# Mixture of experts: 32 slots for the emptier experts, 96 for the two fullest, and a first bias in two single passes

## The chip, the cores and the metric

One core of one Trainium2 chip. The metric is the device time of one execution in microseconds (us), lower is better. A core has TensorE (PE, matmuls; its weight loads are listed apart as PEld), VectorE (DVE), ScalarE (ACT), GpSimd (POOL) and SyncE (SP), whose queue issues most of the DMAs.

## The reference

A network of three blocks on 256 tokens of 1024 features, float32. The change lies in the second block's mixture of experts: 32 experts, four for each token, each expert a gated product of 1024 to 2048 and a product of 1024 to 1024.

```python
logits = (xf @ w_router + b_router)
top_val, top_idx = lax.top_k(logits, TOP_K)          # 4 of 32
gates = jax.nn.softmax(top_val, axis=-1)
...
# for each expert's tokens, each with its gate:
z = x @ w_mlp1[e] + b_mlp1[e]                          # 1024 -> 2048, glu and linear interleaved
glu, lin = min(z[0::2], 7), clip(z[1::2], -7, 7)
y = (glu * sigmoid(1.702 * glu) * (lin + 1)) @ w_mlp2[e] + b_mlp2[e]
```

(The lines behind "..." are the reference's in a short form.) Evaluating the reference's router on its inputs gives the number of tokens of each expert: expert 0 has 13; the other 31 in falling order have 78, 70, 58, 55, 51, 50, 49, 45, 41, 36, 32, 32, 32, 30, 29, 28, 26, 26, 26, 25, 25, 22, 21, 20, 19, 18, 18, 16, 13, 12, 8. The place in that order, from 0 on, is the rank used below: rank 0 has 78 tokens, rank 12 has 32, rank 13 has 30.

## The kernel before

Every expert's weights are read once from HBM: 8 MB for the first product and 4 MB for the second, as twelve DMAs of 1 MB issued by SP (`load`, line 1256). They land in 14 places taken in turn: ten buffers that the whole kernel shares for raw weights (`raw`) and four of the stage's own (`wb`). A load waits in SP's queue until the products that read the place before are done. SP reads each expert's number from SBUF (line 1631) before it issues that expert's loads.

The work is static. Expert 0 comes first, as it needs no ranking, then the others in the order `order`, by ranks that the kernel works out. An expert's tokens are gathered into blocks of 64 slots; the four fullest (`FULL`) have two blocks each, one after the other against the same weights, and all the others one: 36 blocks in all. A loop of run-time length (line 1652) would take what finds no slot.

Per block: `prepare` and `dispatch` make one-hot matrices and gather the rows of four blocks at once (line 1436); `inner` adds the first bias by products of a one-hot of the expert with all the biases (line 1447, float32), then accumulates eight steps of the first product (line 1459). The 64 slots are the stationary operand, so it fills 64 columns of the array; `tile_position` puts two such halves beside each other, each with another quarter of the 2048 outputs, in two PSUM banks. Lines 1466 to 1471 apply the activation, `turned` transposes it (line 1481), `outer` does the second product, again two halves at once (line 1493), and ACT copies it to `y` (line 1496). For every two blocks `close` adds `y`, weighed by the gates, to the 1024 by 256 sums (line 1502).

A float32 product is recorded as two matmul instructions, so the first product of a block is 64 and the second 32. The compiler's scheduler orders the instructions of each engine; the PE order is fixed at build time. In between come products that belong to another stage (the memory's values, line 2449; their weights are fetched into the same places) and the second bias (line 1556). The block before the change needs `b1s`, all first biases, 256 KB, issued behind expert 0's loads (line 1295).

The layer of dense products before (`ffn`, "f11") has room for jobs that need no tokens; `router` is one of them.

Of the kernel before, what the change touches and what calls it, by code (L numbers as in the profile page):

```python
# [19 lines left out]
P = 128  # L20
T = 256
# [15 lines left out]
VALUES = 8  # the rank of the expert after which the first of the memory's values are worked out  # L37
# [4 lines left out]
class Net:  # L42
# [89 lines left out]
    # ---- tokens in, tokens out  # L132
# [51 lines left out]
    # ---- rms norm of the residual with the gain in the matmul's input and the rest left to its output  # L184
# [13 lines left out]
    def square(self, pool, p):  # L198
        """Adds the squares of two of the residual's tiles to the sums by partition."""
# [9 lines left out]
    def add_up(self, acc, tail, update, nxt, pool, fill=()):  # L209
        """The last products of the sums, two tiles of the outputs after the other, and what follows from them."""  # L210
# [12 lines left out]
    def acc_tail(self, acc, tail, p):  # L223
        """The last operand comes last: two pairs of tiles take the others first."""
# [8 lines left out]
    def first_units(self, w, tiles, n=0):  # L233
        """of the next product's first tiles, two for each chunk; the last n of them in slots of the raw weights"""
# [16 lines left out]
    def rstd_start(self):  # L251
        """of the norm that was fed, by tokens [128, 2]"""
# [39 lines left out]
    # ---- weights: raw chunks of up to 8 KB a partition, split in units of 1024 columns  # L292
# [3 lines left out]
    def raw(self, src, k, n, load=True):  # L296
        """src [k*128, n] as [128, k, n]."""
# [5 lines left out]
    def unit(self, src, slot=False):  # L303
        """src [128, a, b] in SBUF, a * b <= 1024 -> float32r parts of the same shape."""
# [12 lines left out]
    def ahead(self, makers, n):  # L317
        """Takes the makers' results in turn, each n places before it is asked for."""
# [62 lines left out]
    # ---- sum over the tiles of K as they come, all of the 1024 outputs open  # L381
# [14 lines left out]
    # ---- swiglu block: x += 0.5 * (silu(h Wg) * (h Wu)) Wo, h = rmsnorm(x)  # L396
# [104 lines left out]
    # ---- chunked spatial gating  # L501
# [89 lines left out]
    # ---- causal means over windows  # L591
    def pool_mixer(self, w_in, w_grp, scale, w_out, nxt):
        nc = self.nc
        Z = 16
        with self.tc.tile_pool(name=self.nm("pm1"), bufs=1) as p1, \
# [15 lines left out]
            # the widest windows first, as they take longest  # L611
# [33 lines left out]
            def evac(i, ps):  # L645
# [8 lines left out]
                if g:  # L654
                    # differences of the running sums
# [21 lines left out]
    # ---- conditioning: mod = silu(c) W + b, one column for each 128 features  # L677
# [43 lines left out]
    # ---- what depends on the positions alone: cos and sin of the rotations, distances of the queries' tiles to all keys  # L721
# [42 lines left out]
    def sin_reduced(self, out, x, tmp, half_out=None):  # L764
        """out = x reduced by whole turns into [-pi, pi]; |x| < 2^22."""
# [32 lines left out]
    def attn_turn(self, pool, pq, causal=True):  # L798
        """pq: probabilities of the two query tiles, [128, n] of one head, turned: keys 0 to 127 of all queries, then the others."""
# [13 lines left out]
    def attn_sum(self, pT, vv, out, causal=True):  # L813
        """out [rows, 256] = v^T p^T"""
# [4 lines left out]
    def gain(self, pool, sc, g):  # L819
        """(1 + sc) * g"""  # L820
# [4 lines left out]
    # ---- the router's matrix with the norm's gain, what the shift gives it, gain and shift by features 8 p + k  # L825
    def route_begin(self, scratch):
# [3 lines left out]
        self.turned_affine = scratch.tile([2, D], F32, name=self.nm("turned_affine"))  # L830

# [22 lines left out]
    # ---- mla and top-k sparse attention on the conditioned norm of the normed residual  # L854
    def attn2(self, V, mod, w_in, w_q_b, w_kv_b, w_o, nxt, mem):
# [6 lines left out]
        with self.tc.tile_pool(name=self.nm("at2"), bufs=2) as p2:  # L862
            # x = u * f * r1, f the first norm's gain, h = x * r2 * g * (1 + sc) + sh
# [16 lines left out]
            def wide(*runs):  # L880
                """128 columns: runs of them"""
# [14 lines left out]
            # low rank parts of the queries, keys and values, and all of the narrow ones, a step behind the input  # L896
# [35 lines left out]
            # the sparse attention's index: queries  # L932
# [16 lines left out]
            # masks: sums in the scores' own accumulation  # L949
# [60 lines left out]
            # queries: nope of two heads in a tile, rope of four  # L1010
# [36 lines left out]
            # attention of two heads at a time, its outputs in the place of the projections' input  # L1047
# [91 lines left out]
            # the last units of the first half of the ring are done with early  # L1139
# [19 lines left out]
    def post_norm(self, pool, acc, tail, g, gate=None, nxt=None, fills=((), (), ()), room=None):  # L1159
        """The last products of the sums, two tiles of the outputs after the other, and x += gate * g * rmsnorm(sums)."""  # L1160
# [76 lines left out]
    # ---- mixture of experts: 64 slots for each expert, 128 for the fullest, and a loop over blocks of 64 where they don't do  # L1237
    def moe(self, V, mod, router, w1, b1, w2, b2, nxt, ahead, mem):
        nc, tc = self.nc, self.tc
        mm = nc.tensor.matmul  # L1240
        E, S, FULL, G = 32, 64, 4, 4
# [7 lines left out]
        # all of the places for weights in turn  # L1249
# [3 lines left out]
        def load(src, n, t):  # L1253
            """one row of 2048 or two of 1024 for each partition"""
# [17 lines left out]
        with self.tc.high_priority():  # L1272
# [5 lines left out]
            iot = self.index(top, [P, S], [[1, S]], 0, 0)  # L1278
            lg = top.tile([P, 2, 40], F32, name=self.nm("lg"))
# [15 lines left out]
        nc.sync.dma_start(b1s, b1)  # L1295
        thi = self.xhi.rearrange("p j t -> p (j t)").rearrange("p (h k q) -> p h k q", h=2, k=KT)
        tlo = self.xlo.rearrange("p j t -> p (j t)").rearrange("p (h k q) -> p h k q", h=2, k=KT)
        with self.tc.high_priority():
# [6 lines left out]
            with self.behind([self.powered]):  # L1305
# [19 lines left out]
                ecol = self.index(p0, [E, 1], [[0, 1]], 0, 1)  # L1325
            for h in range(2):
                nc.vector.scalar_tensor_tensor(lg[:, h, :E], router.logits[:, h, :], r2[:, h:h + 1], self.b_route, op0=ALU.mult, op1=ALU.add)
            # the four highest, their gates, each token's place among its expert's
# [38 lines left out]
        # the last of the memory's keys in between  # L1367
# [3 lines left out]
        # experts 1 to 31 by their numbers of tokens: rank[e], perm[e, r]  # L1371
# [54 lines left out]
        with self.tc.tile_pool(name=self.nm("mo1"), bufs=1, reuse_waits="tile") as p1, \  # L1426
                self.tc.tile_pool(name=self.nm("mo2"), bufs=2, reuse_waits="tile") as p2:
            def dispatch(oh, n):
                """oh: [128, 2, n] one-hot; the chosen rows as [128, k, n]."""
# [11 lines left out]
            def inner(xe, sel, wa, hooks={}):  # L1441
                """xe(k): [128, 64]; sel: [32, 64]; the activations, two runs of 64 slots by 2 x 256."""
                chunk = lambda w, c: w.rearrange("p (q c m) -> p q c m", c=4, m=4)[:, :, c, :]
                pq = [self.bank(), self.bank()]
                for q in range(2):
                    for b in range(2):
                        mm(pq[q][64 * b:64 * b + 64, :], sel, chunk(b1s, 2 * q + b), start=True, stop=False,
                           tile_position=(0, 64 * b), skip_group_check=True)
                together = KT if callable(wa) else 4
# [1286 lines left out]
```

## Time and profile before

| | us |
|---|---|
| median of 3 runs (2836.95 to 2842.62) | 2841.77 |
| profiled execution, span from its first to its last instruction | 2844.6 |
| PE busy in it | 2720.4 (96%) |
| DVE, ACT, POOL busy | 1370.1, 927.5, 221.8 |
| stage of the experts: first load of a ranked expert issued | 1210.05 |
| its last matmul (line 1502) ends | 2317.92 |

The profiled execution has no time but its span; it lies 2.8 us (0.1%) above the median. In the rows below a group shows: line, engine, operation, output<-inputs, shapes, count, busy time in us and mean of one in ns, then idle time before it and what ended it. A busy PE isn't PE at its peak, since matmuls are pipelined and their ends modelled. In the SP rows, L1256 is the line of an expert's loads.

### The profile page before, as it was taken

Reading aid. Unit: us, or ns where it says so; the run is one execution under the profiler, and the core shown is the slowest. Engines: PE = TensorE matmul, PEld = TensorE weight load, DVE = VectorE, ACT = ScalarE, POOL = GpSimd, SP = SyncE. Lnnn points to the kernel's source line nnn. Section 1 sums busy time; section 2 is a strip of 40 time slices with the busy share of each in tenths; the row PEclk is TensorE's granted clock in tenths of the full one; section 3 lists DMA queues with packets and bytes.
Section 4 is the critical chain, followed back from the end, with each engine's and each line's share of the span. In section 5 each row is a group of like instructions: output and inputs, shape, how many; then the busy total and the mean of one; then the engine's idle time right before and its main releaser. Section 6 shows DMA issues by size and latency. Waiting matters only on the chain. (4 is left out here: it accounts for less than half of the span.)

```text
span 2844.6 us, 43953 instructions
## 1 busy us (share of the span) xinstructions
PE 2720.4 (96%) x17739; PEld 1988.0 (70%) x17739; DVE 1370.1 (48%) x2839; ACT 927.5 (33%) x1556; POOL 221.8 (8%) x379
## 2 busy tenths in 40 slices
PE   7999999999999999999999999999999999999998
PEld 7998999999999998844343433333334356799998
DVE  5556676677687768521111112112111138856875
ACT  4445453454454445410000001001001032454654
POOL 0001000010020011200000000000000015301100
PEclk9999999999999999999999999999999999999999
DMA  7855456676557443499988987988988963444540
GB/s 241 304 185 197 164 186 214 207 249 222 194 178 244 165 143 96 179 361 393 391 334 327 407 359 320 420 354 323 414 342 326 409 255 138 132 165 138 189 163 16
DMA packets 272103, 714.22 MB, mean 251 GB/s; under 512 B 13391, under 2 KB 177722, under 8 KB 221690
## 3 DMA queue, kind: packets, MB, share of 16 engines
q1 hardware_dynamic: 269082, 702.32, 66.4%
q0 software_dynamic: 2816, 9.08, 0.9%
q8 instruction: 140, 2.29, 0.3%
q14 instruction: 65, 0.53, 0.1%
HBM read 702.43 MB, written 8.92 MB: 250 GB/s over the span
## 5 line engine op out<-in xcount | busy, mean ns | idle before, releaser
L182 PE MATMUL b<-xhi,hi 128*128 128x256 f32 x2392 | 680.3, 284 | 12.3 <-DVE hi L164 12.1
L180 PE MATMUL b<-xhi,hi 128*128 128x256 f32 x2392 | 685.8, 287 | 6.3 <-ACT xhi L192 5.2
L163 ACT CAST hi<-raw 128x1024 fp32r<-128x1024 f32 (+3 forms) x517 | 509.0, 1002 | 537.0 <-PE b L182 482.3
L181 PE MATMUL b<-xlo,hi 128*128 128x256 f32 x2392 | 680.5, 284 | 3.6 <-DVE xlo L193 2.5
L164 DVE TENSOR_TENSOR hi<-raw,hi 128x1024 fp32r<-128x1024 f32 (+3 forms) x517 | 603.9, 1180 | 157.7 <-ACT hi L163 146.7
L180 PEld LDWEIGHTS b<-xhi,hi 128*128 128x128 f32 x2392 | 456.5, 191 | 21.7 <-issue 7.6
L182 PEld LDWEIGHTS b<-xhi,hi 128*128 128x128 f32 x2392 | 456.4, 191 | 14.8 <-DVE hi L164 14.6
L181 PEld LDWEIGHTS b<-xlo,hi 128*128 128x128 f32 x2392 | 456.7, 191 | 5.6 <-DVE xlo L193 4.5
L1466 DVE TENSOR_SCALAR g<-b 128x256 f32<-128x256 f32 x72 | 30.4, 422 | 839.3 <-PE b L1459 839.3
L1459 PE MATMUL b<-raw,xe 128*64 128x512 f32 x1688 | 384.8, 603 | 0.0
L180 PE MATMUL b<-ahi,hi 128*128 128x256 f32 x1072 | 303.6, 284 | 1.7 <-ACT ahi L163 1.7
L181 PE MATMUL b<-alo,hi 128*128 128x256 f32 x1072 | 302.5, 283 | 2.5 <-DVE alo L164 1.3
L182 PE MATMUL b<-ahi,hi 128*128 128x256 f32 x1072 | 302.0, 282 | 0.8 <-DVE hi L164 0.8
L1459 PEld LDWEIGHTS b<-raw,xe 128*64 128x64 f32 x1688 | 124.8, 138 | 244.2 <-issue 238.6
L1469 ACT ACTIVATE sg<-g 128x256 f32<-128x256 f32 x72 | 30.0, 417 | 556.2 <-DVE g L1466 556.2
L1493 PE MATMUL b<-raw,aT 128*64 128x512 f32 x784 | 202.4, 610 | 8.1 <-DVE aT L1482 3.9
L181 PEld LDWEIGHTS b<-alo,hi 128*128 128x128 f32 x1072 | 203.8, 190 | 3.5 <-DVE alo L164 2.2
L180 PEld LDWEIGHTS b<-ahi,hi 128*128 128x128 f32 x1072 | 203.7, 190 | 3.0 <-ACT ahi L163 2.9
L182 PEld LDWEIGHTS b<-ahi,hi 128*128 128x128 f32 x1072 | 203.9, 190 | 1.0 <-DVE hi L164 1.0
L1496 ACT COPY y<-b 64x512 f32<-64x512 f32 x72 | 41.7, 579 | 355.5 <-PE b L1493 354.8
L1459 PE MATMUL b<-wb,xe 128*64 128x512 f32 x608 | 141.2, 594 | 0.0
L1493 PEld LDWEIGHTS b<-raw,aT 128*64 128x64 f32 x784 | 55.5, 138 | 117.5 <-issue 105.7
(633 smaller groups left out, 3164.8 us busy)
## 6 DMA issues: line engine op xcount, KB each, us to landing
raw<-in_w_mlp_dram SPq DMA_DIRECT2D x275, 1024.0 KB
wb<-in_w_mlp_dram SPq DMA_DIRECT2D x108, 1024.0 KB
raw<-in_ffn_w_in_dram SPq DMA_DIRECT2D x84, 1024.0 KB
raw<-in_ffn_w_out_dram SPq DMA_DIRECT2D x44, 1024.0 KB
raw<-in_w_ada_dram SPq DMA_DIRECT2D x24, 1024.0 KB
raw<-in_ffn_w_up_dram SPq DMA_DIRECT2D x22, 1024.0 KB
raw<-in_w_in_dram SPq DMA_DIRECT2D x21, 1024.0 KB
raw<-in_a_w_in_dram SPq DMA_DIRECT2D x16, 1024.0 KB
```

Of the source, the lines that this page charges most:

```text
L163: a = self.nc.scalar.copy(hi, src)
L164: return a.ins, self.nc.vector.tensor_tensor(lo, src, hi.bitcast(F32), op=ALU.subtract).ins
L180: mm(out, whi, xhi, start=start, stop=False, skip_group_check=True)
L181: mm(out, whi, xlo, start=False, stop=False, skip_group_check=True)
L182: mm(out, wlo, xhi, start=False, stop=stop, skip_group_check=True)
L1459: mm(pq[q][64 * b:64 * b + 64, :], xe(k), chunk(w[:, 0, :], 2 * q + b), start=False, stop=k == KT - 1, tile_position=(0, 64 * b), skip_gro ...
L1466: nc.vector.tensor_scalar(g, v[:, :, 0], 7.0, None, op0=ALU.min)
L1469: nc.scalar.activation(sg, g, AF.Sigmoid, scale=1.702)
L1493: mm(py[64 * c:64 * c + 64, :], aT[:, q, i, b, :], w[:, k % 2, 512 * c:512 * c + 512], start=k == 0, stop=k == KT - 1, tile_position=(0, 6 ...
L1496: nc.scalar.copy(y[64 * z:64 * z + 64, 512 * c:512 * c + 512], py[64 * c:64 * c + 64, :])
```

## The change

1. `FULL` goes from 4 to 2. The two fullest have 96 slots: a block of 64 and a block of 32. Ranks 2 and 3 have one block of 64.
2. Experts from rank `HALF` = 13 on have a block of 32. Its first product uses four column strips of 32 (`inner_half`), each with another quarter of the outputs, all in one bank, and has one activation instead of two; its second product uses four strips too: two halves of the outputs by the even and the odd terms of the sum, whose two partial sums stand in two sets of 32 rows of `y`. The one-hot matrix holds the 32 slots twice (`iot2`), so `close` adds both.
3. Both blocks of the two fullest use each weight tile at once, in step (`also`, and `outer` over a list of blocks).
4. The first bias: `bias_parts`, in the router's job, loads all first biases four times (four DMAs of 256 KB), splits them in two float32r parts on ACT and DVE, and writes 512 KB to DRAM. The experts' stage loads them back ahead of expert 0's weights. A selector (0/1 rows times "is this expert", one DVE operation per block) times the parts gives the bias: two single-pass products of 128 rows per bank.
5. The order: ranks 2 to 9, 0, 10 to 18, 1, 19 to 30; 34 blocks in all.
6. On POOL 16 memsets, a copy and an index more; on PE two small products ahead of expert 0's first product, whose copy on DVE (`who4`) feeds the selectors. The loop's capacity follows the new slots.

Comments and docstrings are gone throughout. The core of the diff:

```diff
-        E, S, FULL, G = 32, 64, 4, 4
+        E, S, FULL, G = 32, 64, 2, 4
+        HALF = 13
...
-            order.insert(7 + 6 * i, i)
+            order.insert(8 + 10 * i, i)
         N = E - 1 + FULL
-        b1s = pb.tile([E, 2048], F32, name=self.nm("b1s"))
+        ranks = [r for r in order for _ in range(2 if r < FULL else 1)]
+        half = [r >= HALF or (c > 0 and ranks[c - 1] == r) for c, r in enumerate(ranks)]
...
+        b1 = pb.tile([P, 2, 512], F32R, name=self.nm("b1"))
+        nc.sync.dma_start(b1.bitcast(F32), self.b1)
         start = weights(w1[0], w2[0], {7: chosen_rows})
-        nc.sync.dma_start(b1s, b1)
...
+    def bias_parts(self, b1):
+        nc = self.nc
+        raw, parts = self.slot(), self.slot(F32R)[:, :1024].rearrange("p (z n) -> p z n", z=2)
+        for c in range(4):
+            nc.sync.dma_start(raw[32 * c:32 * c + 32, :], b1)
+        for c in range(4):
+            r = slice(32 * c, 32 * c + 32)
+            self.split(parts[r, 0, :].rearrange("p (q m) -> p q m", m=4), parts[r, 1, :].rearrange("p (q m) -> p q m", m=4),
+                       raw[r, :].rearrange("p (q c m) -> p q c m", c=4, m=4)[:, :, c, :])
+        nc.gpsimd.dma_start(self.b1, parts.bitcast(F32))
...
+            def inner_half(xe, who, w=None):
+                sel = p2.tile([P, P], F32R, tag="sel2", name=self.nm("sel"))
+                nc.vector.tensor_scalar(sel, quarter.rearrange("p c s -> p (c s)"), who, None, op0=ALU.mult)
+                ps = self.bank()
+                for z in (1, 0):
+                    mm(ps, sel, b1[:, z, :], start=z == 1, stop=False, skip_group_check=True)
+                def step(k, w):
+                    for c in range(4):
+                        mm(ps[32 * c:32 * c + 32, :], xe(k), chunk(w[k][:, 0, :], c), start=False, stop=k == KT - 1,
+                           tile_position=(0, 32 * c), skip_group_check=True)
...
                 for q in range(2):
-                    for b in range(2):
-                        mm(pq[q][64 * b:64 * b + 64, :], sel, chunk(b1s, 2 * q + b), start=True, stop=False,
-                           tile_position=(0, 64 * b), skip_group_check=True)
-                together = KT if callable(wa) else 4
+                    for z in (1, 0):
+                        mm(pq[q], sel[:, q, :], b1[:, z, :], start=z == 1, stop=False, skip_group_check=True)
+                together = KT if callable(wa) or also else 4
...
+                    if also and q == 1:
+                        also(k, wa)
...
+                    for py, (aT, small) in zip(banks, blocks):
+                        for c in range(2):
+                            o, n, x = (64 * c + 32 * i, 32, aT[:, i, k // 2, :]) if small else (64 * c, 64, aT[:, q, i, b, :])
+                            mm(py[o:o + n, :], x, w[:, k % 2, 512 * c:512 * c + 512], start=k < 2 if small else k == 0,
+                               stop=k >= KT - 2 if small else k == KT - 1, tile_position=(0, o), skip_group_check=True)
...
+            who4 = p1.tile([P, N + 1], F32, name=self.nm("who4"))
+            pw = self.bank()
+            mm(pw[:, 0:N], four.rearrange("e a c -> e (a c)"), perm, start=True, stop=True, skip_group_check=True)
...
+                    step, end = inner_half(*rows_of(mine[1]))
+                    acts = [inner(xe, who, wa, also=step), end()]
...
     def router():
         net.route(V, mod[:, 24:32], mod[:, 32:40], I["w_router_2"][0], I["b_router_2"][0])
+        net.bias_parts(I["b_mlp1_2"][0])
```

More of the change, by code (lines that the diff above doesn't have):

```diff
@@ L1325, in moe @@
                 ecol = self.index(p0, [E, 1], [[0, 1]], 0, 1)
+                for t, n in ((quarter, S // 2), (halves.rearrange("p q b s -> p (q b) s"), S)):
+                    for j in range(4):
+                        nc.gpsimd.memset(t[:, j, :], 0.0)
+                        nc.gpsimd.memset(t[32 * j:32 * j + 32, j, :], 1.0)
+                four = p0.tile([E, 4, 32], F32, name=self.nm("four"))
+                nc.gpsimd.tensor_copy(four, self.ident[0:E, 0:E].unsqueeze(1).to_broadcast([E, 4, E]))
             for h in range(2):
@@ new lines, in moe, with end @@
+            chunk = lambda w, c: w.rearrange("p (q c m) -> p q c m", c=4, m=4)[:, :, c, :]
+            def inner_half(xe, who, w=None):
[8 more added lines that the diff above has]
+                           tile_position=(0, 32 * c), skip_group_check=True)
+                def end():
+                    a = p2.tile([P, 2, T], F32, tag="a", name=self.nm("a"))
+                    activate(ps, a[:, 0, :])
+                    return a
+                if w is None:
+                    return step, end
+                for k in range(KT):
+                    step(k, w)
+                return end()
@@ L1444, in inner @@
+            def inner(xe, who, wa, hooks={}, also=None):
+                sel = p2.tile([P, 2, P], F32R, tag="sel2", name=self.nm("sel2"))
+                nc.vector.tensor_scalar(sel, halves.rearrange("p q b s -> p q (b s)"), who, None, op0=ALU.mult)
                 pq = [self.bank(), self.bank()]
                 for q in range(2):
[L1446 to L1448 removed]
@@ L1483, in turned, with outer @@
                 return aT
-            def outer(aT, wb, y, z):
-                py = self.bank()
+            def outer(blocks, wb):
+                banks = [self.bank() for _ in blocks]
                 for k in range(KT):
@@ L1491, in outer, with rows_out @@
                         w = wb(k // 2) if callable(wb) else wb[k // 2]
-                    for c in range(2):
-                        mm(py[64 * c:64 * c + 64, :], aT[:, q, i, b, :], w[:, k % 2, 512 * c:512 * c + 512], start=k == 0,
-                           stop=k == KT - 1, tile_position=(0, 64 * c), skip_group_check=True)
+                    for py, (aT, small) in zip(banks, blocks):
[3 more added lines that the diff above has]
+                               stop=k >= KT - 2 if small else k == KT - 1, tile_position=(0, o), skip_group_check=True)
+                return banks
+            def rows_out(py, y, z):
                 for c in range(2):
@@ L1568, in prepare, with rows_of @@
                     got[c + i] = xe, oh, i
-            def first(c, wa):
+            def rows_of(c):
                 if c not in got:
@@ L1573, in first @@
                 xe, _, i = got[c]
-                return inner(lambda k: xe[:, k, i * S:(i + 1) * S], perm[:, c:c + 1].to_broadcast([E, S]), wa)
-            def second(c, a, wb):
-                z = (c + 1) % 2
-                if c >= 0:
-                    _, oh, i = got.pop(c)
-                if z == 0:
-                    opened[0] = rows()
-                    n = min(2, N - c)
-                    if c >= 0:
-                        opened[1] = back(([oh[:, h, i:i + n].bitcast(F32) for h in range(2)], [gate_r[:, h, c:c + n] for h in range(2)]))
-                elif c == 0:
-                    opened[1] = back(([oh0[:, h:h + 1, :].bitcast(F32) for h in range(2)], [gate[:, h, 0:1] for h in range(2)]),
-                                     ([oh[:, h, i:i + 1].bitcast(F32) for h in range(2)], [gate_r[:, h, c:c + 1] for h in range(2)]))
-                outer(a, wb, opened[0], z)
-                if z == 1 or c == N - 1:
-                    close(opened[0], opened[1], z + 1, c == 0, c == N - 1)
+                return lambda k: xe[:, k, i * S:i * S + (S // 2 if half[c] else S)], who4[:, c:c + 1]
@@ new lines, in first, with second @@
+            def first(mine, wa):
+                if len(mine) == 2:
+                    xe, who = rows_of(mine[0])
+                    step, end = inner_half(*rows_of(mine[1]))
+                    acts = [inner(xe, who, wa, also=step), end()]
+                else:
+                    acts = [(inner_half if half[mine[0]] else inner)(*rows_of(mine[0]), wa)]
+                return acts
+            def second(mine, acts, wb):
+                banks = outer([(a, c >= 0 and half[c]) for c, a in zip(mine, acts)], wb)
+                for c, py in zip(mine, banks):
+                    z = (c + 1) % 2
+                    if c >= 0:
+                        _, oh, i = got.pop(c)
+                    if z == 0:
+                        opened[0] = rows()
+                        n = min(2, N - c)
+                        if c >= 0:
+                            opened[1] = back(([oh[:, h, i:i + n].bitcast(F32) for h in range(2)], [gate_r[:, h, c:c + n] for h in range(2)]))
+                    elif c == 0:
+                        opened[1] = back(([oh0[:, h:h + 1, :].bitcast(F32) for h in range(2)], [gate[:, h, 0:1] for h in range(2)]),
+                                         ([oh[:, h, i:i + 1].bitcast(F32) for h in range(2)], [gate_r[:, h, c:c + 1] for h in range(2)]))
+                    rows_out(py, opened[0], z)
+                    if z == 1 or c == N - 1:
+                        close(opened[0], opened[1], z + 1, c == 0, c == N - 1)
@@ L1593, in moe @@
             a0 = turned(a0)
             prepare(0)
-            second(-1, a0, start[1])
+            second([-1], [a0], start[1])
             def beyond():
-                full = p1.tile([E, 1], F32, name=self.nm("full"))
-                nc.vector.tensor_scalar(full, rank[:, 1:2], float(FULL), None, op0=ALU.is_lt)
-                nc.vector.tensor_scalar(dia, self.ident[:E, :E], full, None, op0=ALU.mult)
+                room = p1.tile([E, 4], F32, name=self.nm("room"))
+                for i, (bound, op, n) in enumerate(((FULL, ALU.is_lt, S // 2), (HALF, ALU.is_ge, -S // 2), (E - 1, ALU.is_ge, S // 2))):
+                    nc.vector.tensor_scalar(room[:, i:i + 1], rank[:, 1:2], float(bound), float(n), op0=op, op1=ALU.mult)
+                nc.vector.tensor_reduce(room[:, 3:4], room[:, 0:3], axis=mybir.AxisListType.X, op=ALU.add)
+                nc.vector.tensor_scalar(dia, self.ident[:E, :E], room[:, 3:4], None, op0=ALU.mult)
@@ L1607, in beyond @@
                 nc.vector.tensor_tensor(more, cnt, base, op=ALU.is_gt)
-                for i in range(1, 3):
+                for i in range(1, 4):
                     nc.vector.scalar_tensor_tensor(t, base, float(S * i), cnt, op0=ALU.add, op1=ALU.is_lt)
@@ L1626, in beyond @@
                 eid = p1.tile([1, 1], I32, name=self.nm("eid"))
-                return ends, key, rest, at, eid
+                ps2 = self.bank()
+                mm(ps2[:, 0:1], four.rearrange("e a c -> e (a c)"), ecol, start=True, stop=True, skip_group_check=True)
+                ecol4 = p1.tile([P, 1], F32, name=self.nm("ecol4"))
+                nc.vector.tensor_copy(ecol4, ps2[:, 0:1])
+                return ends, key, rest, at, eid, ecol4
             c = 0
@@ L1637, in moe @@
                     mem.fetch("v", n)
-                acts = [first(i, wa) for i in mine]
+                acts = first(mine, wa)
                 if c < N and c not in got:
                     prepare(c)
-                for i, a in zip(mine, acts):
-                    second(i, turned(a), wb)
+                second(mine, [(turned_half if half[i] else turned)(a) for i, a in zip(mine, acts)], wb)
                 if r == VALUES - 2:
                     bias()
-                    ends, key, rest, at, eid = beyond()
+                    ends, key, rest, at, eid, ecol4 = beyond()
                 for n in late:
```

57 lines of the change are left out of this document (36 added, 21 removed).

## The prediction

> **What bounds the kernel now.** I read the page's slices first, then stretches of the experts' stage, then its groups of instructions, then what SP's queue waits for. The first lines are the page's slices of PE and DMA (tenths busy, 40 slices of 71 us); the others are stretches of time with the busy time of PE, PEld, DVE, ACT, POOL, then granted clock, DMA share and GB/s.
>
> ```profile
> PE   7999999999999999999999999999999999999998
> DMA  7855456676557443499988987988988963444540
> 1210.00:2318.00 1108.00, 1056.93 (x4667) 412.95 (x4666) 176.39 (x497) 105.64 (x211) 2.65 (x4) 0.99 0.89 360
> 1820.00:1900.00 80.00, 74.47 (x318) 27.58 (x314) 13.94 (x38) 8.50 (x17) 0.00 (x0) 1.00 1.01 421
> 1690.00:1740.00 50.00, 47.52 (x226) 19.48 (x224) 10.20 (x28) 6.51 (x13) 0.00 (x0) 1.00 0.56 222
> ```
>
> PE is busy everywhere. In the experts' stage, 1108 us of the 2844.6, DMA is nearly as full: 0.89. Where experts of one block follow each other (the row 1820 to 1900) it is saturated: share 1.01, 421 GB/s, for 80 us on end. Around an expert of two blocks (1690 to 1740) it falls to 0.56. So two resources lie close together, and which one ends a stretch depends on the blocks per expert. The groups of the stage give PE's price of a block:
>
> ```profile
> L1459 PE MATMUL b<-raw,xe 128*64 128x512 f32 x1610 | 364.8, 600 | 0.0
> L1493 PE MATMUL b<-raw,aT 128*64 128x512 f32 x752 | 192.9, 607 | 7.5 <-DVE aT L1482 3.9 <-issue 2.8 <-ACT sg L1469 0.8
> L1459 PE MATMUL b<-wb,xe 128*64 128x512 f32 x608 | 141.2, 594 | 0.0
> L1447 PE MATMUL b<-b1s,perm 32*64 32x512 f32 x272 | 91.7, 607 | 1.3 <-ACT y L1496 1.3
> L1493 PE MATMUL b<-wb,aT 128*64 128x512 f32 x336 | 82.3, 598 | 1.4 <-DVE aT L1482 1.4
> L1502 PE MATMUL b<-ohT,y 128*128 128x256 f32 x272 | 63.2, 386 | 5.4 <-ACT y L1496 5.4
> L1436 PE MATMUL b<-oh,xhi 128*128 128x256 f32 x128 | 28.3, 297 | 5.5 <-ACT y L1496 4.0 <-DVE a L1467 1.1
> L1436 PE MATMUL b<-oh,xlo 128*128 128x256 f32 x128 | 25.8, 283 | 0.0
> L2449 PE MATMUL b<-raw,m2f 128*128 128x256 f32 x96 | 21.2, 379 | 0.0
> 1248.12 1.17 ACT L1496 COPY y<-b 64x512 f32<-64x512 f32 x2 [6.00 <-PE b L1493]
> 1469.20 1.18 ACT L1496 COPY y<-b 64x512 f32<-64x512 f32 x2 [7.35 <-PE b L1493]
> ```
>
> The window is 1255 to 2301. Per block: first product (364.8 + 141.2) us over 2218/64 blocks = 14.6; second 275.2/34 = 8.1; first bias 91.7/34 = 2.7; sums 63.2/34 = 1.9; gathering (28.3 + 25.8 + 5.5)/32 = 1.9; and some 1.7 of transposes and waits. Groups overlap, so I take the block from the last two rows instead: seven blocks lie between those copies to y, with one job of the memory's values (21.2/3 = 7.1) and the second bias (3.7): (221.1 - 10.8)/7 = 30.0 us. A load of 1 MB (1.0486 million bytes) at 421 GB/s takes 2.49 us, twelve take 29.9. So one block per expert is a tie, and the four experts of two blocks are where DMA loses. The queue and PE agree on who waits:
>
> ```profile
> SPq L1256 <- PE b L1459: 453.3, 227, 22.7
> SPq L1256 <- PE b L1493: 318.0, 111, 15.2
> PEld b L1459 <- DMA raw<-in_w_mlp_dram: 8.1, 27, 0.8
> ```
>
> The loads wait 771 us in the queue for PE to give places back; PE waits 8.1 us for loads, never over 0.8 at once. PE bounds the stage, with DMA close behind.
>
> **The change, part by part.** *Half blocks and strips.* Two strips of 64 run beside each other now. Whether four of 32 do is seen in another stage, whose products (line 695) use four strips over 128 rows:
>
> ```profile
> 450.48 1.92 PE L695 MATMUL b<-raw,sc 128*32 128x512 f32 x16
> 1462.07 7.09 PE L1493 MATMUL b<-wb,aT 128*64 128x512 f32 x32
> 2300.45 0.42 DVE L1466 TENSOR_SCALAR g<-b 128x256 f32<-128x256 f32 x1 [22.62 <-PE b L1459]
> 2301.92 0.41 DVE L1471 TENSOR_TENSOR a<-a,sg 128x256 f32<-128x256 f32 x1
> ```
>
> Sixteen in 1.92 us is 0.12 each; two strips of 64 give 7.09/32 = 0.22. So a half block's products cost half: 14.6/2 = 7.3 and 8.1/2 = 4.05. Its bias is two single passes of 512 columns; line 1436's passes of 256 columns take 54.1/256 = 0.21 us, so 0.42 each, 0.84. Sums 1.9 and gathering 1.9 stay (the gather still makes 64 columns). One activation instead of two leaves nothing to overlap: from the start of line 1466 to the end of line 1471 is 1.9 us, with transposes and copy 3.5. Sum: 19.5 us. That is 10.4 under the 29.9 that its loads need, so in 18 of 32 experts PE stops being the bound and each costs its loads.
>
> *Full blocks:* the bias goes from 2.7 to 4 x 0.42 = 1.7, so 29.0 instead of 30.0. *The two fullest:* 29.0 + 7.3 + 4.05 + 0.84 + 1.9 + 1.9 = 45, instead of 60. *Ranks 2 and 3* lose a block each.
>
> The marks of the stage, by which the sum is made:
>
> ```profile
> 1199.59 0.34 SPq L1295 DMA_DIRECT2D b1s<-in_b_mlp_dram  x1
> 1210.05 3.84 SPq L1256 DMA_DIRECT2D raw<-in_w_mlp_dram  x3
> 1336.86 3.72 PE L1556 MATMUL b<-gT,raw 32*128 32x256 f32 x16
> 2314.20 3.72 PE L1502 MATMUL b<-ohT,y 128*128 128x256 f32 x16 [0.67 <-ACT y L1496]
> ```
>
> *Sum.* Expert 0's y stands at 1248; two small products, a copy and a selector ahead of its first bias make it 1250 (128x256 on DVE is 0.42). Ranks 2 to 9 are full: 8 x 29.0 + 7.1 + 3.7 = 243, to 1493. Rank 0: 1538. Ranks 10 to 12 with two value jobs: 87 + 14, to 1639. Had DMA never stopped since 1210 it could have brought 172 loads by then; PE has used 147 and 14 places hold what is next, so up to here PE bounds and DMA loses some 11 loads. From there 19 experts are left, 228 loads, 14 of them in place: 214 x 2.49 = 533, to 2172. Rank 1 stands in this part: its 45 us put PE 15 us behind, six loads, which the places hold. Behind the last load: its landing 2 (an estimate, under one transfer), last step 0.9, copy and sums 1.2 + 0.7 + 3.7: 2181. Before it was 2314.20 + 3.72 = 2317.9. The gain is 137 us. The stages behind take the 526 us that they took: their first two loads now queue behind the last weights, 5 us, covered by the 6.5 of that tail.
>
> *Bounds.* If DMA never loses a load: 1210 + 375 x 2.49 + 9 = 2153, a gain of 165. If a full block stays at 30.0: 12 us less. If the rate is 400 instead of 421 (the stage's mean now is 360, its saturated stretch 421; I take 421, as no stretch with places free shows less): 214 x 0.13 = 28 less.
>
> *Small parts.* The bias's parts, in the layer before, and the POOL work:
>
> ```profile
> 880.00:940.00 60.00, 60.00 (x507) 58.55 (x506) 43.69 (x129) 23.96 (x33) 4.36 (x6) 1.00 0.69 230
> L2454 ACT COPY mv<-b 128x512 f32<-128x512 f32 x3 | 1.8, 585 | 30.3 <-PE b L2449 30.3
> 1200.41 2.39 POOL L2439 TENSOR_TENSOR m2f<-raw,raw 128x1024 f32<-128x1024 f32 x1
> 1202.75 0.23 POOL L1313 MEMSET skip<- 128x1 f32 x4
> ```
>
> Four splits at 0.6 us are 2.4 us each on ACT and DVE, which are busy 24 and 44 of 60 there while PE never waits; four loads and a store of 1.5 MB meet a DMA share of 0.69. I take 0, up to 5 if the two places they hold delay a layer's load. Sixteen memsets at 0.06 to 0.12 push one m2f sum, not needed before line 2449 at some 1465, and `four`, needed at some 1214: POOL is done near 1206. One move is dangerous: b1's load stands ahead of expert 0's weights on SP, and b1s's was issued only at 1199.59, when its place came free. If b1 waits as long, all twelve weights queue behind it: 1200 + 13 x 2.49 = 1232 for the last, against PE's first product ending near 1235, so expert 0 hardly suffers, and rank 2's loads begin at 1232 instead of 1210, which PE meets at 1250. I take 2 within the 137, at worst 25.
>
> **The rivals.** *A: the clock.* The granted clock can fall inside the stage:
>
> ```profile
> 1344.00:1348.00 4.00, 4.00 (x10) 0.97 (x10) 0.00 (x0) 0.00 (x0) 0.00 (x0) 0.50 1.01 420
> 1352.00:1356.00 4.00, 4.00 (x20) 1.58 (x18) 0.00 (x0) 0.00 (x0) 0.00 (x0) 1.00 1.01 422
> ```
>
> At 0.50 half as many products run in 4 us, behind products of 32 rows only (line 1556 above), with PE never idle. A half block keeps PE a third busy in its first product: 0.9 us of each 2.49. At half clock a half block takes 2 x (7.3 + 4.05 + 0.84 + 1.9 + 1.9 + 0.5) + 2.5 = 35.5 us, over 29.9: 18 x 5.6 = 100 more, 2805. Against it: once PE is behind it works without pauses, and the second row shows 1.00 for dense products. Chance 0.12. The Trainium skill has the rule in "TensorE: Matmul & The Clock Gate", Part 1: the clock halves after an idle window of about 3.4 us. By that rule alone the pauses here, 1.6 us a load, never halve it, and the sum stays 2705; the row at 1344 has the half clock with no idle window, so more than idleness counts here, and the rival stays open.
>
> *B: a later hand-over.* b1 in the way, or full blocks dearer, so that PE's part ends 20 to 45 us later: 2725 to 2750. Chance 0.12.
>
> *C, the other side: slower.* If four strips with interleaved quarters of one weight row don't run together (line 695 reads whole rows), one after the other at 0.43 each (twice the 0.22 of a pair) a half block's products take 64 x 0.43 + 32 x 0.43 = 41 instead of 11.4: 49 us a block. From 37.5 on (29.9 + 137/18) the kernel is slower than before; at 49, with 30 more for ranks 0 and 1 each, the stage ends at 1639 + 30 + 18 x 49 + 75 + 7 = 2633 and the time is near 3155. For strips in pairs a half block costs a full one's 30, and nothing is lost beyond some 20. Chance 0.03, by the row of line 695.
>
> *D: the change doesn't fit the tokens.* Each pass of the loop costs between 29.9 (its loads) and 60 (and a block behind them); three to five passes would undo the gain. By the counts no expert has more tokens than slots (78, 70 against 96; 58 against 64; 30 against 32). Chance 0.02 for slower.
>
> *E: no change.* If the loads' mean of 360 GB/s is a limit of memory and not of places, the stage stays, 2842. The saturated stretch and the queue's 771 us speak against it. Chance 0.03.
>
> **How the numbers follow.** 2844.6 - 137 = 2707.6 for the profiled execution, which stands 2.8 over the median of the runs: 2705, chance 0.68. A change under 0.2% (6 us) can't be told from none. Faster: forecast, A and B, 0.92; same: E, 0.03; slower: C and D, 0.05. The range goes from the bound without a lost load (2842 - 165 = 2677) to the end of B with a few us, 2755; A, C, D and E, 0.20, lie above it.
>
> **What would show it.** Right: the last sums end near 2181; DMA share about 1.0 and 420 GB/s from 1640 on; the queue's waits for PE fall from 771 us to well under half; PE shows waits for weights; products of 128*32 stand 0.12 apart. 68 copies to y. Wrong: a granted clock near 0.5 there with DMA under 0.9 (A), expert 0's first load at 1200 and PE waiting behind it (B), 0.43 between strips (C), loads from the loop's lines (D), saturation under 400 GB/s with SP not waiting (E).

## The result and the profile after

| | before | after |
|---|---|---|
| median, us | 2839.47 | 2731.32 (2729.81 to 2731.86) |
| ratio to before, 95% interval | | 0.962 (0.9607 to 0.9634) |
| profiled execution's span, us | 2844.6 | 2729.1 |
| last matmul of the experts' stage ends, us | 2317.92 | 2200.34 |

The kernel is 3.8% faster. The median lies 26 us above the forecast and inside its range. In the profiled executions, against which the sum was made, 2729.1 stands against 2707.6: 21.5 us of a gain of 137 did not come. The other 5 us come from the step to the median: the forecast took 2.8 off the span, whereas this execution's time, 2731.07, lies 2 above its span. The page's slices show where PE and DMA changed places, PE, then its granted clock, then DMA:

```profile
PE   7999999999999999999999998687676679999998
PEclk8999999999999999989999999799788889999999
DMA  7956455676737662459998899999999973444640
```

From the 25th slice on (1637 us) DMA is full to the end of the stage, and PE has pauses and a lower clock. The stretches of the stage show it in numbers, in the columns used before; the third row is the part of the first behind expert 0's block:

```profile
1211.00:1640.00 429.00, 404.82 (x1839) 171.03 (x1839) 80.83 (x255) 43.06 (x86) 1.98 (x3) 0.98 0.94 380
1640.00:2190.00 550.00, 401.45 (x2343) 128.33 (x2345) 60.84 (x167) 45.41 (x90) 0.67 (x1) 0.84 1.01 421
1260.00:1640.00 380.00, 357.59 (x1615) 145.47 (x1612) 66.33 (x200) 35.63 (x72) 1.37 (x2) 0.99 0.95 389
2200.00:2729.10 529.10, 490.87 (x3630) 452.35 (x3628) 382.22 (x608) 256.01 (x419) 105.42 (x157) 0.96 0.43 145
```

421 GB/s at a share of 1.01 for 550 us on end. What the two sides wait for has turned round:

```profile
SPq L1270 <- DMA raw<-in_w_mlp_dram: 280.0, 152, 2.8
SPq L1270 <- PE b L1523: 131.4, 79, 12.9
SPq L1270 <- DMA wb<-in_w_mlp_dram: 111.0, 60, 2.7
SPq L1270 <- PE b L1565: 85.0, 38, 13.4
PEld b L1491 <- DMA raw<-in_w_mlp_dram: 141.9, 66, 2.4
```

The columns are the waits' total, count and longest. The two waits for PE that made 771 us (line 1459 is 1523 now, 1493 is 1565) make 216; the half blocks' own first products, line 1491, add 26.9. The queue waits 391 us for loads ahead of it. PE's weight loads wait 141.9 us for weights in 66 waits, where it was 8.1. So it looks step by step, late in the stage:

```profile
2149.92 1.07 PE L1491 MATMUL b<-raw,xe 128*32 128x512 f32 x8 [1.42 <-DMA raw<-in_w_mlp_dram]
2152.41 1.07 PE L1491 MATMUL b<-raw,xe 128*32 128x512 f32 x8 [1.43 <-DMA raw<-in_w_mlp_dram]
2154.89 1.07 PE L1491 MATMUL b<-raw,xe 128*32 128x512 f32 x8 [1.42 <-DMA raw<-in_w_mlp_dram]
...
2184.72 1.93 PE L1491 MATMUL b<-raw,xe 128*32 128x512 f32 x8 [1.42 <-DMA raw<-in_w_mlp_dram]
2189.85 6.07 PE L1565 MATMUL b<-raw,aTh 128*32 128x512 f32 x32 [0.56 <-issue]
2196.62 3.72 PE L1578 MATMUL b<-ohT,y 128*128 128x256 f32 x16 [0.69 <-ACT y L1572]
```

Eight products in strips of 32 take 1.07 us, and the next eight start 2.49 us later, when the next load has landed. The copies to `y` give the marks of the sum: expert 0, the last of ranks 2 to 9, rank 0's second block, rank 12, the last of all.

```profile
1252.56 1.17 ACT L1572 COPY y<-b 64x512 f32<-64x512 f32 x2 [6.00 <-PE b L1565]
1496.66 1.17 ACT L1572 COPY y<-b 64x512 f32<-64x512 f32 x2 [6.75 <-PE b L1565]
1544.57 1.17 ACT L1572 COPY y<-b 64x512 f32<-64x512 f32 x2 [3.60 <-PE b L1578]
1637.82 1.18 ACT L1572 COPY y<-b 64x512 f32<-64x512 f32 x2 [11.00 <-PE b L1565]
2195.99 1.18 ACT L1572 COPY y<-b 64x512 f32<-64x512 f32 x2 [8.39 <-PE b L1565]
```

The forecast had 1250, 1493, 1538, 1639 and some 2176. Up to rank 12 it holds within 7 us. The last mark agrees better than the work does: of the three jobs of the memory's values that the sum put ahead of rank 12's copy, the third came behind it:

```profile
1642.00 7.07 PE L2552 MATMUL b<-raw,m2f 128*128 128x256 f32 x32
```

So for the same work PE was some 6 us late. The larger error lies behind that.

### The profile page after: what moved, and what is told of

Same layout as the page of the kernel before. It is cut to its first block, busy times and chain, and to the rows that moved or that the text cites. A ratio compares the mean times of both kernels' runs of the same rounds, so it can differ in the third digit from the quotient of the medians.

```text
span 2729.1 us, 42924 instructions
## 1 busy us (share of the span) xinstructions
PE 2480.5 (91%) x17295; PEld 1879.3 (69%) x17295; DVE 1339.8 (49%) x2770; ACT 917.1 (34%) x1531; POOL 222.9 (8%) x392
## 5 line engine op out<-in xcount | busy, mean ns | idle before, releaser
L1472 DVE TENSOR_SCALAR g<-b 128x256 f32<-128x256 f32 x48 | 20.3, 423 | 611.0 <-PE b L1491 382.6
L1475 ACT ACTIVATE sg<-g 128x256 f32<-128x256 f32 x48 | 20.0, 417 | 539.7 <-DVE g L1472 538.8
L1491 PE MATMUL b<-raw,xe 128*32 128x512 f32 x944 | 145.9, 719 | 60.0 <-DMA raw<-in_w_mlp_dram 59.5
L1491 PEld LDWEIGHTS b<-raw,xe 128*32 128x32 f32 x944 | 23.0, 117 | 170.5 <-DMA raw<-in_w_mlp_dram 141.9
L1523 PE MATMUL b<-raw,xe 128*64 128x512 f32 x616 | 139.9, 600 | 0.0
L452 DVE TENSOR_TENSOR t<-b,rb 128x256 f32<-128x256 f32 x88 | 37.2, 423 | 169.8 <-PE b L182 169.4
L1523 PEld LDWEIGHTS b<-raw,xe 128*64 128x64 f32 x616 | 43.7, 138 | 85.7 <-issue 82.7
```

Source lines behind the costliest of these rows:

```text
L452: nc.vector.tensor_tensor(t, ps[:, :T], rb, op=ALU.mult)
L1472: nc.vector.tensor_scalar(g, v[:, :, 0], 7.0, None, op0=ALU.min)
L1475: nc.scalar.activation(sg, g, AF.Sigmoid, scale=1.702)
L1491: mm(ps[32 * c:32 * c + 32, :], xe(k), chunk(w[k][:, 0, :], c), start=False, stop=k == KT - 1, tile_position=(0, 32 * c), skip_group_check ...
L1523: mm(pq[q][64 * b:64 * b + 64, :], xe(k), chunk(w[:, 0, :], 2 * q + b), start=False, stop=k == KT - 1, tile_position=(0, 64 * b), skip_gro ...
```

## The experiments

The theory to test: halves make the loads the bound from rank 13 on, and the 21.5 us are loads that DMA failed to bring while PE was the bound (ranks 2 to 12), because a place that PE gives back is not yet a place that holds weights. Each result below gives the median, then its ratio to the kernel before with a 95% interval; the changed kernel's median is 2731.32.

**Halves undone.** All ranked experts but the two fullest's second blocks go back to 64 slots.

```diff
-        HALF = 13
+        HALF = 31
```

> All ranks from 2 on get a block of 64 again (HALF = 31); the two fullest keep 64 + 32 with shared tiles, and the new bias stays. Theory (from about 1640 on the loads end the stage, at 29.9 us an expert, so the half blocks' PE time is mostly not on the path): ranks 2 to 9 took (1496.7 - 1252.6 - 10.8)/8 = 29.2 us a full block, so the 18 ranks and rank 1 take 18 x 29.2 + 48 instead of the 556 us up to the last copy: 19 us more, about 2750. Rival (the halves carry the gain, 9.7 us of PE each): 18 x 9.7 = 175 more, about 2905.

2761.87 us, 0.9739 (0.9715 to 0.9762): 12 us above the theory, far from the rival. From rank 12's copy to the last one (1634.65 to 2231.48) it took 597 us, where the theory had 574. In the part of the halves:

```profile
1640.00:2230.00 590.00, 548.59 (x2425) 208.56 (x2425) 93.95 (x257) 52.89 (x108) 0.67 (x1) 0.99 0.97 396
```

PE is 93% busy and DMA still reaches 396 GB/s. With a block at 29.2 us against the loads' 29.9 the tie holds without halves too; they brought 31 us. The other 77 come from the rest (two fewer blocks, second blocks of 32 for the two fullest, the bias), which this run does not separate.

**Only loads.** The experts from rank 13 on load no second weights, and use their first tiles 4 to 7 in that place.

```diff
-            wb = [load(b[:, 2 * u:2 * u + 2, :], D, place()) for u in range(4)]
+            wb = [load(b[:, 2 * u:2 * u + 2, :], D, place()) if second else wa[4 + u].rearrange(...) for u in range(4)]
```

> Experts from rank 13 on don't load their second weights; the second product reads the last four tiles of the first (that part of the result is left out). All products stay. Theory (loads end that part): an expert costs the larger of 8 x 2.49 = 19.9 and PE's own 19.5 to 22, so 18 x 8 to 10 less: 2551 to 2587. Rival (PE itself, at the granted clock of 0.84, ends that part): no more than a few us less, 2725 or over.

2568.71 us, 0.9047 (0.903 to 0.9064). Four of twelve loads less in 18 experts are 72 x 2.49 = 179 us, and the time fell by 163. The loads are the bound there. And the block in halves has its upper bound: from rank 12's copy to the last one, ranks 13 to 30 and rank 1:

```profile
1636.50 1.18 ACT L1572 COPY y<-b 64x512 f32<-64x512 f32 x2 [11.00 <-PE b L1565]
2034.16 1.18 ACT L1572 COPY y<-b 64x512 f32<-64x512 f32 x2 [1.55 <-PE b L1565]
```

They take 397.7 us; less 45 for rank 1 it is 19.6 for a half block, where eight loads need 19.9 and the forecast had 19.5.

**First products twice.** Every half block of an expert with one block does each step of its first product a second time, so that PE works more between loads.

```diff
                 for k in range(KT):
                     step(k, w)
+                    step(k, w)
```

> Single half blocks take each step of the first product twice (the result is not the reference's there): 7.3 us more of PE for each of 18 experts, no load more. Theory (loads end that part): 19.5 + 7.3 = 27 us is still under 29.9, so 2731 to 2740. Rival (PE ends it): 18 x 7.3 = 131 more, about 2862.

2730.08 us, 0.9621 (0.9603 to 0.9639), a microsecond under the theory's range: 18 times 64 more recorded products cost nothing that can be measured.

```profile
1640.00:2190.00 550.00, 469.78 (x3493) 163.92 (x3496) 60.73 (x167) 45.38 (x90) 0.67 (x1) 0.96 1.01 420
```

PE works 68 us longer in the same stretch, and its clock is 0.96 instead of 0.84. So the low clock in the changed kernel comes with the pauses, and costs nothing, as the loads set the pace at either clock.

**Another order.** Half blocks and full ones alternate up to rank 23, so that PE never bounds for long.

```diff
-        order = list(range(FULL, E - 1))
+        order = [x for i in range(11) for x in (HALF + i, FULL + i)] + list(range(HALF + 11, E - 1))
...
-            order.insert(8 + 10 * i, i)
+            order.insert(8 + 11 * i, i)
...
```

> Full and half blocks alternate (ranks 13, 2, 14, 3, ... 23, 12, then 24 to 30, with ranks 0 and 1 between), everything else as in the changed kernel. Theory (PE bounds the first part, loads the second, and what DMA loses in the first is never made up): a pair costs PE 29.2 + 19.5 = 49 against 60 us of loads, so the three dips of the DMA share after 1260 (8.8 + 10 + 3.4 us) go: about 2709. Rival (the dips are the price of single events, such as the block pair or the value jobs): 2725 to 2731.

2704.08 us (2698.75 to 2706.61), 0.9525 (0.9507 to 0.9542).

```profile
1260.00:1640.00 380.00, 335.16 (x1716) 120.92 (x1708) 61.91 (x196) 36.53 (x73) 0.00 (x0) 0.94 1.01 419
1640.00:2160.00 520.00, 422.83 (x2196) 151.00 (x2192) 63.36 (x179) 44.45 (x88) 2.04 (x3) 0.89 1.01 419
```

419 GB/s instead of 389 from 1260 to 1640 is 380 us x 30 GB/s = 11.4 MB, 11 loads, 27 us, as much as the medians differ by. The profiled executions, 29.5 us apart, add up too: the stretch before brings two loads more, as DMA ran at 355 GB/s there against 310, and the one behind, at 419 against 421, brings one less.

```profile
1211.00:1260.00 49.00, 44.77 (x266) 20.54 (x269) 16.35 (x69) 7.84 (x15) 0.62 (x1) 0.94 0.91 355
```

What DMA loses in the first part is paid at the end, load for load.

**Two places fewer.**

```diff
-        p3, pb = pool("mo3", 4), pool("mob")
+        p3, pb = pool("mo3", 2), pool("mob")
...
-        places = itertools.cycle([self.slot] * 7 + [own] * 4 + [self.slot] * 3)
+        places = itertools.cycle([self.slot] * 7 + [own] * 2 + [self.slot] * 3)
```

> 12 places for weights instead of 14 (two of the stage's own fewer). Theory (how many loads stand ready when the loads become the bound is set by the places beyond the twelve of the expert in work): two loads fewer at the hand-over, 5 us, and more lost in the part that PE bounds: 2736 to 2756. Rival (places don't matter, the rate does): 2731.

2734.6 us, 0.9626 (0.961 to 0.9642), just under the lower end and within what one kernel's runs differ by. Its expert 0 ended 8 us earlier (copy at 1244.62) and its last copy came 2 us later, so what two places are worth stays open, between the medians' 3 us and the 10 between those two copies. It is not the 21.5: the sum was wrong less in how many places there are than in how many of them are full.

**The old first bias.** The float32 products over 32 rows return, four for each full block; the half blocks have theirs in strips of 32.

```diff
-                    for z in (1, 0):
-                        mm(pq[q], sel[:, q, :], b1[:, z, :], start=z == 1, stop=False, skip_group_check=True)
+                    for b in range(2):
+                        mm(pq[q][64 * b:64 * b + 64, :], who.to_broadcast([E, S]), chunk(b1s, 2 * q + b), start=True, stop=False,
+                           tile_position=(0, 64 * b), skip_group_check=True)
...
-        net.bias_parts(I["b_mlp1_2"][0])
...
```

> The first bias by float32 products of 32 rows as before, no bias parts, no selectors, b1s behind expert 0's loads; half blocks take it in four strips. Theory (PE time counts only before about 1640): 2.7 - 1.35 = 1.35 us for each of expert 0, ranks 2 to 12 and rank 0's two blocks, 14 x 1.35 = 19 more, less up to 6 for an earlier first product of expert 0: 2744 to 2750. Rival (PE time counts in all 34 blocks): up to 40 more, 2771.

2753.39 us, 0.9689 (0.9673 to 0.9705): 22 us slower than the changed kernel, 3 above the theory and far from the rival. The bias on PE as a group, over 11 full blocks, in this kernel and then in the changed one:

```profile
L1503 PE MATMUL b<-b1s,perm 32*64 32x512 f32 x88 | 29.3, 605 | 0.0
```

```profile
L1512 PE MATMUL b<-b,sel 128*128 128x512 f32 x44 | 14.8, 438 | 0.0
```

2.66 us a block against 1.35. Rank 12's copy stands 20 us later (1657.67); from there to the last copy it takes 564 us, against 558. So PE time added ahead of the hand-over comes out at the end about one for one. The run with halves from rank 10 on, below, shows that PE time saved there need not.

**The two fullest's blocks one after the other.**

```diff
-                    step, end = inner_half(*rows_of(mine[1]))
-                    acts = [inner(xe, who, wa, also=step), end()]
+                    acts = [inner(xe, who, wa), inner_half(*rows_of(mine[1]), wa)]
...
-                banks = outer([(a, c >= 0 and half[c]) for c, a in zip(mine, acts)], wb)
+                banks = [outer([(a, c >= 0 and half[c])], wb)[0] for c, a in zip(mine, acts)]
```

> The two fullest experts' blocks of 64 and 32 take the weights one after the other instead of tile by tile. PE's products are the same. Theory (what counts is when places come free): rank 0's eight first tiles come free only in the second block, some 13 us later, and DMA loses about that before 1640; rank 1's loss falls in the part where loads end the stage and can't be made up either: 2740 to 2757. Rival (the same products, the same time): 2731.

2725.34 us (2722.77 to 2729.22), 0.9597 (0.9581 to 0.9613): 6 us faster than the changed kernel where 9 to 26 more were expected, a miss. But the trace shows that the edit did less than it says. The scheduler still put rank 0's two first products tile by tile on PE (line 1523 for the block of 64, line 1491 for the block of 32), as in the changed kernel, and rank 1's nearly so. Only the second products (line 1565) stand apart:

```profile
1491.08 1.89 PE L1523 MATMUL b<-wb,xe 128*64 128x512 f32 x8
1492.90 1.07 PE L1491 MATMUL b<-wb,xe 128*32 128x512 f32 x8
1493.89 1.94 PE L1523 MATMUL b<-wb,xe 128*64 128x512 f32 x8
...
1517.30 7.07 PE L1565 MATMUL b<-raw,aT 128*64 128x512 f32 x24
1528.00 2.78 PE L1565 MATMUL b<-raw,aTh 128*32 128x512 f32 x22
```

So the theory, that the first tiles' places come free late and DMA loses loads by it, was not tested. What was tested is the second product. From the last full block's copy to rank 0's last one it takes 44.0 us (1491.35 to 1535.39), against 47.9 in the changed kernel (1496.66 to 1544.57). The first products take 22.9 us in both; the second take 13.5 (1517.30 to 1530.78) against 17.4 in step (1522.76 to 1540.19), which is the whole difference. In step, four products of 32 slots between those of 64 take as long as eight of them elsewhere, as if only two strips ran beside each other:

```profile
1529.18 1.05 PE L1565 MATMUL b<-raw,aTh 128*32 128x512 f32 x4
```

That is 0.26 each; the 22 in a row above take 0.13 each. So second products in step gain nothing on PE, they cost 4 us. Expert 0's copy also stands at 1244.04 here, 8.5 us earlier, and the last copy 8.1 us earlier (2187.93 against 2195.99). The stretch ahead of expert 0's copy, in the changed kernel and then in this one:

```profile
1205.00:1220.00 15.00, 15.00 (x72) 14.41 (x72) 8.29 (x31) 3.34 (x10) 3.89 (x9) 0.50 0.59 216
```

```profile
1205.00:1220.00 15.00, 14.21 (x79) 9.14 (x80) 7.77 (x37) 3.38 (x6) 0.61 (x1) 0.82 0.68 247
```

PE runs at half clock in the one and at 0.82 in the other, on work that the edit does not touch. This is not all of the 8.5 us. PE's first product on the token masks, ahead of the stretch, already starts 4.3 us later in the changed kernel, here first, than in this run:

```profile
1204.47 0.38 PE L1387 MATMUL b<-mask,before 128*128 128x32 f32 x2 [1.88 <-DVE mask L1369]
```

```profile
1200.13 0.59 PE L1387 MATMUL b<-mask,before 128*128 128x32 f32 x2 [1.88 <-DVE mask L1369]
```

The last four runs take up how much the start is worth.

**Halves from rank 10 on.**

```diff
-        HALF = 13
+        HALF = 10
```

> Blocks of 32 from rank 10 on (ranks 10 to 12 have 32 tokens each). Theory: three blocks fewer of 29.2 and more of 19.5 in the part that PE bounds; it ends 29 us earlier, but the loads can only gain what DMA loses there behind rank 0, 3 to 13 us: 2718 to 2728. Rival (each us of PE counts): 29 less, 2702. Rival (none counts): 2731.

2721.91 us, 0.9581 (0.9565 to 0.9597), as expected: the hand-over comes three experts earlier, and of 29 us less on PE 9 reach the end. Ranks 10 to 12 have exactly 32 tokens, so nothing is dropped. Part of these 9 us may be the start (copy at 1246.81).

**The bias's load behind expert 0's weights, and the changed kernel once more.**

```diff
-        nc.sync.dma_start(b1.bitcast(F32), self.b1)
         start = weights(w1[0], w2[0], {7: chosen_rows})
+        nc.sync.dma_start(b1.bitcast(F32), self.b1)
```

> The load of the bias's parts is issued behind expert 0's twelve weight loads instead of ahead of the last of them. Theory 1 (in the changed kernel this load, held up for a place until 1202.6, delayed only the one load behind it; the late end of expert 0's first block there, 1252.6 against 1244 to 1247 in several variants, comes from the clock's 0.50 in 1210 to 1220): 2729 to 2733, no difference beyond 2 us, apart from the start, which may fall either way by up to 8. Rival (the load ahead costs the start itself): copies to y of expert 0 at 1244 to 1247 and 2723 to 2726.

> The changed kernel once more, unaltered, for the spread between chips and builds. If the late start (clock 0.50 in 1210 to 1220, expert 0's copy to y at 1252.6) belongs to the program, the time is 2731 within 2 and the copy stands at 1252 again; if it is chance of an execution, some run falls to 2722 to 2726 and the copy to 1244 to 1247.

2730.06 us, 0.9609 (0.9596 to 0.9622), and 2730.34 us, 0.9612 (0.9596 to 0.9628). The load's place costs nothing that can be measured. The unaltered kernel's five runs reach from 2724.73 to 2734.34, so the 6 us of the run with the second products apart are not told from none. Both profiled executions have the half clock and a copy at 1252 (1251.96 and 1252.20). In both PE comes to the token masks as late as in the changed kernel (1203.88 and 1204.12), so the half clock is not the whole of the late start there either. That the shortest of these runs are those with an early start is possible, but no profile of one shows it, and the run with the first products twice speaks against it: its copy stands at 1247.32, yet it took 2729.58 us. This stays open, as does what starts the half clock.

**The mixed order again**, with the bias's load behind, and with the edit that was to put the two fullest's blocks one after the other; the edits are those shown.

> The mixed order of ranks (a half block behind each full one) with the bias's load behind expert 0's weights. If the load's place costs nothing: 2699 to 2706 as the mixed order alone. If it costs the start 6 to 8 us: 2692 to 2698.

> The mixed order of ranks, with the two blocks of the two fullest one after the other, each reading the weights by itself. Theory (sharing brings nothing; the 6 us of the variant with sharing undone were its start, which the mixed order alone has already): 2699 to 2707, as the mixed order alone. Rival (sharing itself costs 6 us, by both blocks' ends falling together): 2693 to 2698.

2702.36 us, 0.9517 (0.9504 to 0.953), and 2701.58 us, 0.9515 (0.9502 to 0.9528). With the mixed order alone at 2704.08 the three can't be told apart: neither the load's place nor second products in step or apart matter. Sharing the first tiles stays untested, as rank 0's first products stand tile by tile here too. The mixed order beats both kernels, about 1% under the changed one and 4.8% under the one before.

## Why the prediction was right in kind and 21 us short

- **The mis-sized term: "14 of them in place".** At 1640 PE has used 147 loads (with the one of the value job at 1642.00), and the sum took 161 as landed. The load behind the step at 2184.72 is the 371st of 375 (four of second weights follow). At 2.49 us each, 219 landed from 1640 to it, so some 152 had landed by 1640: 5 in place, not 14. (The step at 1696.61, the first to wait for its load, is the 176th; counted back from there it is 6.) In place of 533 us the rest took (2194.7 - 1640) = 555, with the last load at 2184.72 + 4 x 2.49 = 2194.7. These 22 us are the miss. The queue shows why:

```profile
1635.57 19.65 SPq L1270 DMA_DIRECT2D raw<-in_w_mlp_dram  x10
...
2159.94 15.24 SPq L1270 DMA_DIRECT2D raw<-in_w_mlp_dram  x7
2177.28 13.88 SPq L300 DMA_DIRECT2D raw<-in_w_in_dram  x2
```

  The last load of an expert is issued by 2175.18 and lands at 2194.7, 19.5 us later: the time of 7.8 loads, so that many are on the way, itself among them. Counted in the queue's rows from 1211.04 on, some 156 loads of ranked experts are issued by 1640, and PE has used 144 of them: 12 places hold an order, 5 of them weights. The prediction's own numbers said so: a full block of 29.0 us gives DMA no time to refill at 29.9.
- **Lost loads.** From 1260 to 1640 they are 380 x (421 - 389) / 1048.6 = 11.6, the 11 of the forecast. Before that, 1211 to 1260, DMA ran at 310 GB/s (the rows' difference: (429 x 380 - 380 x 389) / 49), 5 loads fewer than at 421, and carried the last of expert 0's own. Those the sum did not have.
- **Full block:** (1496.66 - 1252.56 - 10.8) / 8 = 29.2 for 29.0. **The fullest:** 47.9 for 45. The sum had 8.1 + 4.05 = 12.15 for its second products, with the block of 32 in four strips at once; in step they took 17.4, and apart 13.5. **Half block:** 19.6 at most, for 19.5; four strips of 32 in a row run together at 0.13 (1.07/8), so rival C is out. Rank 12 came at 1637.8 for 1639, but with a value job of 7.1 still to do that the sum had ahead of it. That the hand-over's mark came out within 1 us is luck: PE was some 6 us late, 2.6 of it at the start and 2.9 at rank 0.
- **The rate:** 421 GB/s held for 550 us, so rival E is out.
- **Tail and stages behind:** from the last load 5.6 us (2200.34 - 2194.7) for 9; then 528.8 (2729.1 - 2200.34) for 526.6, likely as the next stage's first weights queue behind, which no run here singles out. Together with the 22 and the mark of 1640 for the sum's 1639: 21.7 + 1 - 3.4 + 2.2 = 21.5.
- **The bias's parts and `b1`.** The load did wait, to 1202.63, but only one of expert 0's loads stood behind it, not twelve, since the rest had been issued; the first ranked load came at 1211.04 for 1210.05, and moving it gained nothing. The time measured lies in rival B's 2725 to 2750, but not by its mechanism: PE's part ended some 6 us late, not 20 to 45.
- **Rival A** foresaw the clock's fall, which the forecast did not have: 0.84 in the part of the halves, some steps at half clock (1.93 us for 8, above). Its price was wrong: even at 1.93 a step ends before the next load, 2.49, and PE, busy 401 of 550 us, catches up behind it. That the loop never ran (68 copies to `y`) settles D.

PE's longest wait from 1640 to 2190, ahead of the transposes, then the longest for weights, on PE and on its weight loads:

```profile
PE b L1538 <- DVE a L1477: 27.3, 18, 2.0
PE b L1491 <- DMA wb<-in_w_mlp_dram: 25.4, 21, 1.8
```

```profile
PEld b L1491 <- DMA wb<-in_w_mlp_dram: 51.9, 27, 2.7
```

The Trainium skill, "TensorE: Matmul & The Clock Gate", Part 1, has the clock halve after an idle window of some 3.4 us; here no wait of PE is longer than 2.0 us, none of its weight loads for weights longer than 2.7, and the mean clock was 0.84, where by the window alone it would be 1. The same page, under "A second HAM failure mode", tells of a clock that oscillates from short pauses between groups of products; the 0.96 that came with twice the products agrees with that.

## What to carry to other kernels

Where two resources lie within a few per cent of each other, halving the work of one on part of the items only moves the bound there; order the items so that each stretch has the same ratio of both, and the second one never stops: here the order alone brought 27 us, and halving 31. For a queue that fills places, count at a hand-over what has landed, not what has been given back: a full queue holds its depth in transfers on the way. Before reading 6 us out of a variant, run the same kernel again, and see in the trace whether the scheduler kept the order that the edit meant.

## Not expected of the hardware

- PE at half clock with no idle time in it: 15.00 of 15.00 us busy at 0.50 from 1205 to 1220, in some executions and not in others of nearly the same program.
- Four products in strips of 32 take 1.05 us between products in strips of 64, as long as eight in a row (1.07).
- One kernel's runs differ by 9.6 us (2724.73 to 2734.34), more than the first four runs showed (2 us).
- A load of 1 MB lands some 19.5 us after its issue when the queue is saturated, against 2.49 us of transfer.
